# A conformer block and two mixer layers on one core: another order for the first block's transfers and steps, earlier tap sums, products of zeros at the start, and a last quarter taken token tile by token tile

## The chip, the core and the metric

The kernel runs on one core of a Trainium2 chip. The metric is the device time of one execution in microseconds (us), the median of several runs. TensorE (PE) multiplies, VectorE (DVE) and ScalarE (ACT) do the work on elements, GpSimd (POOL) does little here, and SyncE (SP) only issues transfers. Each of these engines takes its instructions in the order in which they are written.

## What is computed

A first block (conformer convolution and an MLP), then two layers of a second model, on 256 tokens of width 1024, in float32. The change touches the first block alone, up to its second pointwise product. Cut to that:

```python
mod = silu(c) @ w_mod + b_mod                        # w_mod 1024 x 6144, 24 MB
sh1, s1, g1, sh2, s2, g2 = split(mod, 6)
hl = rms_norm(x, norm1_g) * (1 + s1) + sh1
u = hl @ w_pw1 + b_pw1                               # w_pw1 1024 x 2048
a, gate = split(u, 2)
u = a * sigmoid(gate)
u = dwconv(u in 4 segments of 64, w_dw) + b_dw       # 31 taps
u = silu(layer_norm(u, ln_g, ln_b))
y = u @ w_pw2 + b_pw2
x = x + g1 * y
x = x + g2 * (square(relu((rms_norm(x, norm2_g) * (1 + s2) + sh2) @ w1)) @ w2)
```

## The kernel before

**Weights.** Every weight comes in one stream of transfers of up to 1 MB on SP's queue, in the order of a plan (`PLAN`). Weights that are split into a rounded part and a rest go into one of three `raw` buffers (2048 columns, so two chunks of 1024); ACT makes `hi` (L408), DVE makes `lo` (L425), and the last `lo` of a buffer frees it. `W.get` and `W.ahead` keep the split two chunks ahead of the products. The pieces of `w_mod` are not split; they go into one of four `home` buffers of 1 MB (home0, home1 and the two halves of home2), and a home is free when its reader is done. SP issues in the plan's order: a transfer whose buffer is not yet free holds back every one behind it.

**The modulation.** F0 to F3 (two transfers each) hold the columns of sh1 and s1 for a quarter of the channels, D0 to D3 those of s2, P0 to P7 those of g1 and sh2, R0 to R3 those of g2. F, P and R are multiplied on PE (`mod_chunk`, four products of 32 rows, L744). ACT then copies the row (`modrow`, L754), and small products turn it into columns (`mod_columns`, `mod_cols`). D is multiplied and summed on DVE (`mod_dots`, two instructions, L782).

**The first pointwise product.** The 16 chunks c0 to c15 each hold two blocks of 128 x 512. A block is multiplied for two token tiles t with three products each (L915 to L917): 12 products per chunk, accumulated in `gated[q][t]` for the four column quarters q. Chunks 0 to 11 go channel pair by channel pair over q = 0, 1, 2 and need the modulated input of F0, F1, F2, F3 in turn (`modulated(c)`, called M); chunks 12 to 15 are q = 3. When a quarter has its last block, `glu(q)` (ACT `sg`, DVE L873) frees its banks and starts `conv`: products `x_ps` (L890), DVE products with the tap sums `wf` (L893), products `c_ps` (L897), a copy to `cb` (L902) and statistics (L903).

**Order.** Two strings set it: `TRANSFERS` the plan's first part, `PW1_STEPS` the order of steps. Generators in `bg` are advanced by one at each `slot()`. After the steps come P6, P7 and R0 to R3, then the layer norm of `cb`, eight transposes with SiLU (`ln_act`), and the second pointwise product `pw2` (L700 to L702): four steps of 24 products, then `finish`.

**Tap sums.** `tap_sums` (two products L821, each followed by an ACT copy L822) runs behind c0. Its source row is then overwritten by `c_row`, which the dots need.

Of the kernel before, what the change touches and what calls it, by code (L numbers as in the profile page):

```python
# [27 lines left out]
RANK = 1 + 3 * NFREQ  # L28
# [14 lines left out]


TRANSFERS = (
    "F0 c0 F1 c1,2 c3 F2 c4,5 D0 F3 c6,7 P0 D1 c8,9 P1 D2 c10,11 P2 P3 D3 c12,13 P4 P5 c14,15 P6 P7 w0,1 R0 R1 w2,3 R2 R3 "
    "w4,5,6,7"
)
PW1_STEPS = (
    "c0 F1 c1 M1 c2 c3 F2 c4 M2 c5 D0 c6 F3 c7 M3 c8 P0 D1 c9 P1 D2 c10 P2 c11 D3 P3 c12 P4 c13 P5 c14 c15"  # L50
)


# [423 lines left out]
def tile_conformer_then_mixer(ctx: ExitStack, tc: tile.TileContext, stream, xT, pT, vec, con, rows_in, taps, c_row, out):  # L477
# [11 lines left out]
    def bank(name):  # L489
        return pp_.tile([P, 512], F32, tag="b", name=name)  # L490
# [59 lines left out]
    def slot():  # L550
        step(stages)
        step(bg)

    def drain():
        while bg:
            slot()
# [287 lines left out]
    normed(0, 2)  # L844
    for _ in work:
        pass
    pw1_bias(2)

    def modulated(c):
# [11 lines left out]
            nc.vector.tensor_sub(xs[:, k, T:], xn[:, k, :], xs[:, k, :T])  # L861

    modulated(0)
    normed(2, KB)

    czb = rows1[:, :D]


    def glu(q):
        for t in range(2):  # L870
            sg = tp.tile([P, T], F32, tag="t256", name="sg", bufs=6)
            nc.scalar.activation(sg, gated[q][t][:, 256:], AF.Sigmoid)
# [11 lines left out]
    def conv(t, c0, c1):  # L884
# [17 lines left out]
        nc.scalar.copy(cb[:, t, c0:c1], o[:, :n])  # L902
        nc.vector.bn_stats(stats[:, t, max(c0 // 256 - 1, 0), :], o[:, :n])  # L903

    def pw1_chunk(i):
        hi, lo = W.get(("pw1", 0, i))
        for j in range(2):
            q, k = PW1[2 * i + j]
            if k == 0 and q not in gated:
                pw1_bias(q)  # L910
            s = slice(512 * j, 512 * j + 512)
            for t in range(2):
                xh, xl = (xs[:, k, T * part + P * t : T * part + P * t + P] for part in range(2))
                kw = dict(start=False, skip_group_check=True)
                nc.tensor.matmul(gated[q][t], xh, hi[:, s], stop=False, **kw)  # L915
                nc.tensor.matmul(gated[q][t], xh, lo[:, s], stop=False, **kw)
                nc.tensor.matmul(gated[q][t], xl, hi[:, s], stop=(k == KB - 1), **kw)  # L917
# [22 lines left out]

    works = {}
    for item in PW1_STEPS.split():
        taken(item[0], int(item[1:]))
        if item == "c0":
            tap_sums()
            nc.sync.dma_start(czb, c_row.to_broadcast([P, D]))
        elif item == "c2":
# [54 lines left out]
    mv_ = tp.tile([P, 2, 2], F32, tag="lnmv", name="lnmv", bufs=1)
    rstd = tp.tile([P, 2], F32, tag="rt", name="rstd")
    for t in range(2):
        nc.vector.bn_aggr(mv_[:, t, :], stats[:, t].rearrange("p a b -> p (a b)"))
    rsqrt_(rstd, mv_[:, :, 1], 1.0)
    nc.scalar.preload_act_table_set("silu_and_others")
    for c in range(2):
        for t in range(2):
            part = cb[:, t, 512 * c : 512 * c + 512]  # L1010
            nc.vector.tensor_scalar(part, part, mv_[:, t, 0:1], rstd[:, t : t + 1], ALU.subtract, ALU.mult)
# [16 lines left out]
    pw2 = Mixed("pw2", 0, xs, PW2_EARLY, PW2_LATE, ev_pw2)  # L1028
    acts = {}

    def ln_act(k):
        ps = bank("tr_ps")
        for t in range(2):
            nc.tensor.transpose(ps[:, P * t : P * t + P], cb[:, t, P * k : P * k + P], ident)
        n = acts[k] = tp.tile([P, T], F32, tag="t256", name="lnx", bufs=6)
        nc.scalar.activation(n, ps[:, :T], AF.Silu, scale=V("ln_g", k, 1), bias=V("ln_b", k, 1))

    for k in range(KB + 2):
        if k < KB:
# [12 lines left out]
        if j == 4:  # L1052
            bg.append(bias_rows())
# [667 lines left out]
```

## Time and profile before

| what | value |
|---|---|
| median of 3 runs | 1061.83 us (1057.67 to 1063.64) |
| the profiled execution, its own time | 1061.67 us |
| its span, first to last instruction | 1059.9 us |
| PE busy | 1015.3 us, 96% |
| DVE busy | 752.7 us, 71% |
| ACT busy | 593.0 us, 56% |
| DMA | 192.9 MB, mean 182 GB/s |

A busy PE is not PE at its best: the page also gives the clock that it was granted, and its products take about twice as long at the lower of two levels. The chain of waits is followed back from the last instruction; its rows tell which work ended last in each stretch. For a transfer two things count: when SP could issue it, and how long it took to land.

### The profile page before, as it was taken

Reading aid. Unit: us, or ns where it says so; the run is one execution under the profiler, and the core shown is the slowest. Engines: PE = TensorE matmul, PEld = TensorE weight load, DVE = VectorE, ACT = ScalarE, POOL = GpSimd, SP = SyncE. Lnnn points to the kernel's source line nnn. Section 1 sums busy time; section 2 is a strip of 40 time slices with the busy share of each in tenths; the row PEclk is TensorE's granted clock in tenths of the full one; section 3 lists DMA queues with packets and bytes.
Section 4 is the critical chain, followed back from the end, with each engine's and each line's share of the span. In section 5 each row is a group of like instructions: output and inputs, shape, how many; then the busy total and the mean of one; then the engine's idle time right before and its main releaser. Section 6 shows DMA issues by size and latency. Waiting matters only on the chain.

```text
span 1059.9 us, 16455 instructions
## 1 busy us (share of the span) xinstructions
PE 1015.3 (96%) x6386; PEld 875.8 (83%) x6386; DVE 752.7 (71%) x1445; ACT 593.0 (56%) x1070; POOL 101.8 (10%) x86
## 2 busy tenths in 40 slices
PE   6878899999999999999999999999999999999996
PEld 3554488988888989898888888998989888888896
DVE  5245347785788779886888875467997788887545
ACT  5332366553565644767555554674576765554555
POOL 0000004000003200002000002520000200000243
PEclk9888979999999999899999999999999999999998
DMA  9669625555555543334555555454343455555541
GB/s 375 257 267 368 267 93 185 209 198 175 186 192 168 181 154 106 126 131 140 194 197 199 180 179 198 155 188 132 140 147 122 134 190 194 195 174 187 198 160 40
DMA packets 28416, 192.90 MB, mean 182 GB/s; under 512 B 3368, under 2 KB 3757, under 8 KB 6961
## 3 DMA queue, kind: packets, MB, share of 16 engines
q1 hardware_dynamic: 26784, 188.32, 49.6%
q0 software_dynamic: 784, 1.99, 0.7%
q10 hardware_dynamic: 770, 1.54, 0.4%
q8 instruction: 50, 0.82, 0.3%
q14 instruction: 28, 0.23, 0.1%
HBM read 190.78 MB, written 2.04 MB: 182 GB/s over the span
## 4 chain that ended last, share of the span: by engine, by line
PE 77%; DVE 8%; ACT 4%; issue 1%; DMA 1%; DVEq 0%; ACTq 0%
PE g_ps L638 33%; PE g_ps L639 17%; PE mx_ps L700 3%; PE mx_ps L702 3%; PE g_ps L631 3%; PE mx_ps L701 3%; PE g_ps L632 2%; PE g_ps L633 2%; DVE lo L425 2%; ACT hi L408 1%; PE o_ps L1380 1%; PE pt_ps L1417 1%; PE cs_ps L616 1%; DMA home<-stream 1%; DVE big_a L1358 1%
## 5 line engine op out<-in xcount | busy, mean ns | idle before, releaser
L408 ACT CAST hi<-raw 128x1024 fp32r<-128x1024 f32 (+2 forms) x310 | 320.5, 1036 | 308.1 <-PE g_ps L638 148.8
L425 DVE TENSOR_TENSOR lo<-raw,hi 128x1024 fp32r<-128x1024 f32 (+2 forms) x294 | 361.0, 1230 | 143.2 <-ACT hi L408 142.2
L638 PE MATMUL g_ps<-xf,hi 128*128 128x512 f32 x704 | 247.0, 395 | 0.0
L639 PE MATMUL g_ps<-xf,lo 128*128 128x256 f32 x704 | 197.4, 280 | 0.0
L638 PEld LDWEIGHTS g_ps<-xf,hi 128*128 128x128 f32 x704 | 132.0, 187 | 30.9
L639 PEld LDWEIGHTS g_ps<-xf,lo 128*128 128x128 f32 x704 | 133.0, 189 | 0.1
L638 PE MATMUL g_ps<-big_f,hi 128*128 128x512 f32 x352 | 124.4, 397 | 0.0
L639 PE MATMUL g_ps<-big_f,lo 128*128 128x256 f32 x352 | 99.1, 281 | 0.0
L638 PE MATMUL g_ps<-big,hi 128*128 128x512 f32 x256 | 90.5, 397 | 0.0
L638 PEld LDWEIGHTS g_ps<-big_f,hi 128*128 128x128 f32 x352 | 66.1, 188 | 16.3
L639 PE MATMUL g_ps<-big,lo 128*128 128x256 f32 x256 | 72.1, 282 | 0.0
L638 PE MATMUL g_ps<-xs_h,hi 128*128 128x512 f32 x192 | 67.0, 393 | 0.0
L639 PEld LDWEIGHTS g_ps<-big_f,lo 128*128 128x128 f32 x352 | 66.4, 189 | 0.0
L638 PEld LDWEIGHTS g_ps<-big,hi 128*128 128x128 f32 x256 | 48.1, 188 | 11.8
L639 PE MATMUL g_ps<-xs_h,lo 128*128 128x256 f32 x192 | 53.8, 280 | 0.0
L602 POOL TENSOR_TENSOR accP<-accP,sq 128x256 f32<-128x256 f32 x12 | 17.7, 1479 | 331.0 <-ACT sq L601 331.0
L639 PEld LDWEIGHTS g_ps<-big,lo 128*128 128x128 f32 x256 | 48.3, 188 | 0.1
L631 PE MATMUL g_ps<-xs_l,hi 128*128 128x256 f32 x144 | 42.9, 298 | 0.0
L638 PEld LDWEIGHTS g_ps<-xs_h,hi 128*128 128x128 f32 x192 | 36.0, 187 | 8.1
L632 PE MATMUL g_ps<-xs_l,lo 128*128 128x256 f32 x144 | 41.7, 290 | 0.7 <-DVE lo L425 0.7
L631 PE MATMUL g_ps<-xn,hi 128*128 128x256 f32 x144 | 41.8, 290 | 0.0
L633 PE MATMUL g_ps<-xs_l,hi 128*128 128x256 f32 x144 | 41.6, 289 | 0.0
(360 smaller groups left out, 2245.9 us busy)
## 6 DMA issues: line engine op xcount, KB each, us to landing
raw<-stream SPq DMA_DIRECT2D x142, 1024.0 KB, 4.8
home<-stream SPq DMA_DIRECT2D x24, 1024.0 KB, 8.6
raw<-stream SPq DMA_DIRECT2D x4, 904.0 KB, 4.5
raw<-stream SPq DMA_DIRECT2D x4, 768.0 KB, 4.5
raw<-stream SPq DMA_DIRECT2D x2, 896.0 KB, 4.4
raw<-stream SPq DMA_DIRECT2D x2, 784.0 KB, 4.3
h<-xT SPq DMA_DIRECT2D x1, 1024.0 KB, 6.7
raw<-stream SPq DMA_DIRECT2D x2, 512.0 KB, 11.4
```

Of the source, the lines that this page charges most:

```text
L408: self.nc.scalar.copy(hi[:, : PLAN[i][1]], raw)
L425: eng.tensor_sub(lo[:, :w], raw, hi[:, :w])
L602: nc.gpsimd.tensor_add(acc, acc, s)
L616: nc.tensor.matmul(ps[:, :T], ones, part, start=(i == 0), stop=(i == len(parts) - 1))
L631: nc.tensor.matmul(ps, hi, xs[:, k, :T], start=first, stop=False)
L632: nc.tensor.matmul(ps, lo, xs[:, k, :T], start=False, stop=False)
L633: nc.tensor.matmul(ps, hi, xs[:, k, T:], start=False, stop=last)
L638: nc.tensor.matmul(ps, hi, xs[:, k, :], start=first, stop=False, skip_group_check=True)
L639: nc.tensor.matmul(ps[:, :T], lo, xs[:, k, :T], start=False, stop=last, skip_group_check=True)
L700: nc.tensor.matmul(ps, hi[:, s], xs[:, k, :T], start=first and m < 4, stop=False, **kw)
L701: nc.tensor.matmul(ps, lo[:, s], xs[:, k, :T], start=False, stop=False, **kw)
L702: nc.tensor.matmul(ps, hi[:, s], xs[:, k, T:], start=False, stop=last, **kw)
```

## The change

- `TRANSFERS` and `PW1_STEPS` are written anew. F3 now comes before c6,7 and the D, P and R pieces later: between c7 and c12 the steps take D0 to D3, between c11 and c15 P0 to P3, behind c15 P4 to P7. The order in which a home is used is now the order in which it was filled.
- R0 to R3 are taken in a generator `gate1` among the products of `pw2`.
- `tap_sums` does both products first, behind the columns of F0 and ahead of c0, and copies later; the `c_row` transfer is written ahead of c0. Loading the rest of the constants moves from c7 to c4, the sigmoid of `c_row` from c2 to c5.
- At the start PE gets four products of zeros (128 x 512, `WARM`), whose result is not read, and DVE a memset for them.
- c15 is multiplied token tile by token tile (`pw1_last`); `glu(3)` starts behind the first, each tile's convolution behind its own gate, and each tile has its own norm (`token_norm`).

```diff
-    "F0 c0 F1 c1,2 c3 F2 c4,5 D0 F3 c6,7 P0 D1 c8,9 P1 D2 c10,11 P2 P3 D3 c12,13 P4 P5 c14,15 P6 P7 w0,1 R0 R1 w2,3 R2 R3 "
+    "F0 c0 F1 c1,2 c3 F2 c4,5 F3 c6,7 D0 c8,9 D1 D2 c10,11 D3 P0 c12,13 P1 P2 P3 c14,15 P4 P5 w0,1 P6 P7 R0 w2,3 R1 R2 R3 "
     "w4,5,6,7"
-    "c0 F1 c1 M1 c2 c3 F2 c4 M2 c5 D0 c6 F3 c7 M3 c8 P0 D1 c9 P1 D2 c10 P2 c11 D3 P3 c12 P4 c13 P5 c14 c15"
+    "c0 F1 c1 M1 c2 F2 c3 c4 M2 c5 F3 c6 c7 M3 D0 c8 c9 D1 c10 D2 c11 D3 P0 c12 P1 c13 P2 c14 P3 c15"
...
+    nc.vector.memset(u[:, 0, :512], 0.0)
+    idle_ps = bank("idle_ps")
+    for _ in range(WARM):
+        nc.tensor.matmul(idle_ps, u[:, 0, :P], u[:, 0, :512], start=True, stop=True)
...
+    sums = tap_sums()
+    next(sums)
     pw1_bias(2)
...
     modulated(0)
+    for _ in sums:
+        pass
     normed(2, KB)
...
+    nc.sync.dma_start(czb, c_row.to_broadcast([P, D]))
...
+            if q == 3:
+                bg.append(conv(t, 256 * q, 256 * q + 256))
             yield
...
+    def pw1_last(i):
+
+        hi, lo = W.get(("pw1", 0, i))
+        for t in range(2):
+            for j in range(2):
+                pw1_products(hi, lo, i, j, t)
+            if t == 0:
+                W.ahead()
+                bg.append(glu(3))
+            slot()
...
+    taken("P", 4)
     slot()
+    taken("P", 5)
     slot()
     taken("P", 6)
+    slot()
+    norm0 = token_norm(0)
+    next(norm0)
+    slot()
+    drain()
     taken("P", 7)
-    slot()
     work = mod_columns("pair", 2)
-    next(work)
-    taken("R", 0)
-    taken("R", 1)
-    slot()
-    slot()
-    taken("R", 2)
-    taken("R", 3)
...
+    def gate1():
+        taken("R", 0)
+        yield
+        taken("R", 1)
+        yield
+        taken("R", 2)
+        yield
+        taken("R", 3)
+        bg.append(mod_columns("one", 5))
...
+    bg.append(gate1())
     for k in range(KB + 2):
```

SP's queue from the row for the dots (`c_row`) on, before. Line 394 is the stream; home2 stands for both halves of the third home buffer. In this order the rows are D0 and F3a, F3b, c6,7, P0, D1, c8,9, P1, D2, c10,11, the constants, P2.

```order
L946 DMA big0_84<-c_row 128x1024
L394 DMA home2_93<-stream 128x2048 x2
L394 DMA home0_91<-stream 128x2048
L394 DMA raw13_311<-stream 128x2048
L394 DMA home1_92<-stream 128x2048
L394 DMA home2_93<-stream 128x2048
L394 DMA raw16_367<-stream 128x2048
L394 DMA home2_93<-stream 128x2048
L394 DMA home0_91<-stream 128x2048
L394 DMA raw19_396<-stream 128x2048
L952 DMA cons_81<-con 128x1664
L394 DMA home1_92<-stream 128x2048
```

The same stretch of SP's queue now: F3a and F3b, c6,7, D0, c8,9, D1, the constants, D2, c10,11, D3, P0, c12,13.

```order
L881 DMA big0_84<-c_row 128x1024
L395 DMA home2_93<-stream 128x2048 x2
L395 DMA raw12_247<-stream 128x2048
L395 DMA home0_91<-stream 128x2048
L395 DMA raw14_301<-stream 128x2048
L395 DMA home1_92<-stream 128x2048
L977 DMA cons_81<-con 128x1664
L395 DMA home2_93<-stream 128x2048
L395 DMA raw17_378<-stream 128x2048
L395 DMA home2_93<-stream 128x2048
L395 DMA home0_91<-stream 128x2048
L395 DMA raw20_435<-stream 128x2048
```

F3 moved ahead of D0, and P0 behind all four D; c12,13 stand behind P0, which takes D0's buffer.

DVE from the columns of M3 on, now. Line 426 makes `lo`, 788 is a dot (two for each D), 888 the product with the gate; raw14 holds c8,9, raw17 c10,11, raw20 c12,13.

```order
L426 TENSOR_TENSOR lo18_418<-raw14_301,hi18_404 128x1024
L781 TENSOR_TENSOR mods_116<-mod_cols_117,vecs_80 128x2x2
L864 SCALAR_TENSOR_TENSOR G1_146<-mods_116,vecs_80 128x2
L873 TENSOR_TENSOR xs_h1_90<-big0_84,xs_h1_90 128x256 x2
L788 SCALAR_TENSOR_TENSOR home0_91,mods_116<-home0_91,big0_84 128x1024 x2
L426 TENSOR_TENSOR lo21_451<-raw17_378,hi21_437 128x1024
L426 TENSOR_TENSOR lo22_467<-raw17_378,hi22_453 128x1024
L888 TENSOR_TENSOR big0_84<-g_ps_147,sg_469 128x256
L788 SCALAR_TENSOR_TENSOR home1_92,mods_116<-home1_92,big0_84 128x1024 x2
L888 TENSOR_TENSOR big0_84<-g_ps_148,sg_483 128x256
L426 TENSOR_TENSOR lo25_492<-raw20_435,hi25_475 128x1024
L888 TENSOR_TENSOR big0_84<-g_ps_153,sg_494 128x256
```

Behind these rows stand D2, a gate product, the `lo` of c13, a gate product, D3. Before, D0 stood ahead of the columns of M3 and D2 ahead of the `lo` of c12; now each stands behind.

PE at the end of the stretch, before: the last convolution, R0 to R3 (line 744, R0 and R1 on home0 and home1, R2 and R3 on home2), the columns of P, the transposes.

```order
L890 MATMUL x_ps<-big_84,cons 118x256 x4
L744 MATMUL mod_ps<-home_91,cz 32x512 x4
L744 MATMUL mod_ps<-home_92,cz 32x512 x4
L897 MATMUL c_ps<-big_84,cons 64x256 x4
L744 MATMUL mod_ps<-home_93,cz 32x512 x8
L761 MATMUL mod_cols<-cons,modrow 128x4 x4
L1034 MATMUL tr_ps<-cons,big_84 128x128 x6
L700 MATMUL mx_ps<-xs_ln,hi_631 128x256
```

Now, where line 750 with home_91, home_92 and twice home_93 is P4 to P7, and the last one on home_91 is R0.

```order
L907 MATMUL x_ps<-big_84,cons 118x256 x2
L750 MATMUL mod_ps<-home_91,cz 32x512 x4
L907 MATMUL x_ps<-big_84,cons 118x256 x2
L750 MATMUL mod_ps<-home_92,cz 32x512 x4
L914 MATMUL c_ps<-big_84,cons 64x256 x2
L750 MATMUL mod_ps<-home_93,cz 32x512 x4
L914 MATMUL c_ps<-big_84,cons 64x256 x2
L750 MATMUL mod_ps<-home_93,cz 32x512 x4
L767 MATMUL mod_cols<-cons,modrow 128x4 x4
L1076 MATMUL tr_ps<-cons,big_84 128x128 x6
L750 MATMUL mod_ps<-home_91,cz 32x512 x4
L706 MATMUL mx_ps<-xs_ln,hi_620 128x256
```

R1 to R3 moved in among the products of `pw2`, and the columns of P no longer stand behind an R.

## Rows read from the trace of the kernel before

**Rows 1.** The page's first line, and the clock granted to PE in 40 equal slices of the span, in tenths of the full one.

```profile
span 1059.9 us, 16455 instructions
...
PEclk9888979999999999899999999999999999999998
```

**Rows 2.** Busy time of each engine by stretch (us from the span's start: length; PE, PEld, DVE, ACT, POOL with their counts; then the granted clock, the DMA share and GB/s).

```profile
27.00:60.00 33.00, 28.93 (x137) 18.52 (x138) 11.81 (x18) 12.29 (x18) 0.00 (x0) 0.86 0.54 202
60.00:90.00 30.00, 23.12 (x102) 14.54 (x100) 10.80 (x17) 6.98 (x11) 0.00 (x0) 0.89 0.88 357
90.00:121.00 31.00, 27.75 (x102) 13.98 (x106) 17.61 (x29) 9.84 (x17) 0.00 (x0) 0.83 0.76 298
...
136.00:154.00 18.00, 18.00 (x115) 17.66 (x116) 6.94 (x11) 8.94 (x17) 0.00 (x0) 0.74 0.17 58
...
170.00:1059.00 889.00, 875.33 (x5706) 786.14 (x5706) 676.93 (x1309) 522.54 (x954) 95.69 (x76) 0.99 0.48 167
```

**Rows 3.** The chain of waits between 102 and 136 us: start, time that this piece took in the chain, what.

```profile
102.70 0.43 PE g_ps L916
...
104.66 0.99 PE mod_ps L744 x8
...
106.33 0.23 PE g_ps L917
...
107.26 1.92 PE c_ps L897 x8
...
115.45 1.01 PE c_ps L897 x8
...
120.78 1.90 PE mod_ps L744 x16
...
122.70 6.31 DMA home<-stream
...
129.06 1.06 PE mod_ps L744 x8
130.12 1.00 PE mod_cols L761 x8
...
133.46 0.95 PE tr_ps L1034 x2
...
135.80 0.58 PE mx_ps L700
```

**Rows 4.** SP's queue in order of time: start of the first issue, time to the end of the last one in the row, what is issued, how many. The first is the row for the dots; the homes in the others are D0, F3a and F3b; P0 and D1; P2, P3 and D3.

```profile
26.52 0.33 SPq L946 DMA_DIRECT2D big<-c_row  x1
29.16 13.24 SPq L394 DMA_DIRECT2D home<-stream  x3
...
42.97 16.22 SPq L394 DMA_DIRECT2D home<-stream  x2
...
75.60 5.05 SPq L394 DMA_DIRECT2D home<-stream  x3
```

**Rows 5.** What SP's issues waited for in the first 160 us: total us, times, longest.

```profile
SPq L394 <- PE mod_ps L744: 54.5, 10, 13.6
SPq L394 <- DVE home L782: 31.5, 4, 15.4
SPq L394 <- DVE lo L425: 30.7, 3, 22.9
```

**Rows 6.** Issues of transfers between 113.8 and 114.2 us, with what is moved, its size and the us from issue to landing: one, with nothing else under way.

```profile
home<-stream SPq DMA_DIRECT2D x1, 1024.0 KB, 4.8
```

**Rows 7.** The same between 29.0 and 29.3 us: D0, issued while `c_row` was still under way.

```profile
home<-stream SPq DMA_DIRECT2D x1, 1024.0 KB, 7.1
```

**Rows 8.** The stretch from 15 to 30 us, in which transfers followed each other without a gap (columns as in Rows 2).

```profile
15.00:30.00 15.00, 12.77 (x46) 6.04 (x45) 8.18 (x17) 5.70 (x10) 0.00 (x0) 0.75 1.01 418
```

**Rows 9.** The beginning in order of time: start, length, engine, line, what, in brackets the idle time before and what ended it. The first is F0 on PE, then the split of c0, the columns of F0, the first product with c0, the second tap sum, F1.

```profile
10.85 3.86 PE L744 MATMUL mod_ps<-home,cz 128*32 128x512 f32 x16
...
14.02 1.05 ACT L408 CAST hi<-raw 128x1024 fp32r<-128x1024 f32 x1 [2.31 <-DMA raw<-stream]
...
15.62 1.03 PE L771 MATMUL mod_cols<-cons,modrow 128*128 128x1 f32 x8
...
18.49 0.50 PE L915 MATMUL g_ps<-hi,xs_h 128*128 128x512 f32 x1 [0.73 <-ACT xs_h L856]
...
25.10 1.38 PE L821 MATMUL wf_ps<-big,cons 31*118 31x512 f32 x2 [0.68 <-ACT big L822]
...
27.16 3.64 PE L744 MATMUL mod_ps<-home,cz 128*32 128x512 f32 x16 [0.68 <-ACT big L822]
```

**Rows 10.** DVE's groups between 16 and 136 us: line, engine, operation, names and shapes, count, then busy us, mean ns of one, idle time before and what ended it.

```profile
L425 DVE TENSOR_TENSOR lo<-raw,hi 128x1024 fp32r<-128x1024 f32 x18 | 21.9, 1222 | 38.4 <-ACT hi L408 38.4
L782 DVE SCALAR_TENSOR_TENSOR home<-home,big 128x1024 f32<-128x1024 f32 x8 | 9.4, 1217 | 0.0
...
L873 DVE TENSOR_TENSOR big<-g_ps,sg 128x256 f32<-128x256 f32 x8 | 3.3, 420 | 10.7 <-ACT sg L872 10.6
...
L893 DVE TENSOR_TENSOR big<-x_ps,big 118x512 f32<-118x512 f32 x4 | 2.5, 679 | 0.0
```

**Rows 11.** ACT's groups of the same stretch, with the same columns.

```profile
L408 ACT CAST hi<-raw 128x1024 fp32r<-128x1024 f32 x17 | 17.6, 1045 | 49.2 <-DMA raw<-stream 39.9 <-issue 4.9 <-PE g_ps L917 4.4
L859 ACT ACTIVATE big<-big,mods,G 128x256 f32<-128x256 f32 x6 | 3.6, 599 | 6.6 <-DVE G L852 6.6
```

More of the change, by code (lines that the diff above doesn't have):

```diff
@@ L35 @@
 EPS = 1e-6
+WARM = 4
 NEG = -1.0e30
@@ L817, in tap_sums @@
     def tap_sums():
+        pss = [bank("wf_ps") for _ in range(2)]
         for c in range(2):
-            ps = bank("wf_ps")
-            nc.tensor.matmul(ps[:RANK], C("at")[:TAPS], rows1[:TAPS, 512 * c : 512 * c + 512], start=True, stop=True)
-            nc.scalar.copy(wf[:RANK, 512 * c : 512 * c + 512], ps[:RANK])
+            nc.tensor.matmul(
+                pss[c][:RANK], C("at")[:TAPS], rows1[:TAPS, 512 * c : 512 * c + 512], start=True, stop=True
+            )
+        yield
+        for c in range(2):
+            nc.scalar.copy(wf[:RANK, 512 * c : 512 * c + 512], pss[c][:RANK])
     for q in range(2):
@@ L876, in glu @@
             ln_exp()
-        if q > 0:
+        elif q > 0:
             c0 = 0 if q == 1 else 256 * q
@@ L903, in conv, with pw1_products @@
         nc.vector.bn_stats(stats[:, t, max(c0 // 256 - 1, 0), :], o[:, :n])
+    def pw1_products(hi, lo, i, j, t):
+        q, k = PW1[2 * i + j]
+        s = slice(512 * j, 512 * j + 512)
+        xh, xl = (xs[:, k, T * part + P * t : T * part + P * t + P] for part in range(2))
+        kw = dict(start=False, skip_group_check=True)
+        nc.tensor.matmul(gated[q][t], xh, hi[:, s], stop=False, **kw)
+        nc.tensor.matmul(gated[q][t], xh, lo[:, s], stop=False, **kw)
+        nc.tensor.matmul(gated[q][t], xl, hi[:, s], stop=(k == KB - 1), **kw)
     def pw1_chunk(i):
@@ L910, in pw1_chunk @@
                 pw1_bias(q)
-            s = slice(512 * j, 512 * j + 512)
             for t in range(2):
[L913 to L917, printed above, removed]
+                pw1_products(hi, lo, i, j, t)
             if k == KB - 1:
@@ L922, in pw1_chunk @@
             slot()
+    def pw1_last(i):
+        hi, lo = W.get(("pw1", 0, i))
+        for t in range(2):
+            for j in range(2):
+                pw1_products(hi, lo, i, j, t)
+            if t == 0:
+                W.ahead()
+                bg.append(glu(3))
+            slot()
     def taken(kind, i):
         if kind == "c":
-            pw1_chunk(i)
+            (pw1_last if i == 15 else pw1_chunk)(i)
         elif kind == "F":
@@ L943, in tile_conformer_then_mixer @@
         taken(item[0], int(item[1:]))
[L944 to L947, printed above, removed]
+        if item == "c4":
+            nc.sync.dma_start(cons[:, CON_FIRST:], con[:, CON_FIRST:])
+        elif item == "c5":
             nc.scalar.activation(u[:, 0, :], czb, AF.Sigmoid)
-        elif item == "c3":
+        elif item == "c6":
             nc.vector.tensor_mul(czb, czb, u[:, 0, :])
-        elif item == "c7":
-            nc.sync.dma_start(cons[:, CON_FIRST:], con[:, CON_FIRST:])
         elif item == "c10":
@@ L955, in tile_conformer_then_mixer, with token_norm @@
     nc.vector.tensor_add(mods[:, 4, :], mods[:, 4, :], V("b_mod", 4 * KB, KB))
+    mv_ = tp.tile([P, 2, 2], F32, tag="lnmv", name="lnmv", bufs=1)
+    rstd = tp.tile([P, 2], F32, tag="rt", name="rstd")
+    def token_norm(t):
+        nc.vector.bn_aggr(mv_[:, t, :], stats[:, t].rearrange("p a b -> p (a b)"))
+        rsqrt_(rstd[:, t : t + 1], mv_[:, t, 1:2], 1.0)
+        yield
+        for c in range(2):
+            part = cb[:, t, 512 * c : 512 * c + 512]
+            nc.vector.tensor_scalar(part, part, mv_[:, t, 0:1], rstd[:, t : t + 1], ALU.subtract, ALU.mult)
+    taken("P", 4)
     slot()
+    taken("P", 5)
     slot()
     taken("P", 6)
+    slot()
[3 more added lines that the diff above has]
+    drain()
     taken("P", 7)
-    slot()
     work = mod_columns("pair", 2)
-    next(work)
-    taken("R", 0)
-    taken("R", 1)
-    slot()
-    slot()
-    taken("R", 2)
-    taken("R", 3)
+    norm1 = token_norm(1)
+    next(norm1)
+    for n in (norm0, norm1):
+        for _ in n:
+            pass
     for _ in work:
         pass
-    drain()
-    bg.append(mod_columns("one", 5))
-    slot()
+    nc.scalar.preload_act_table_set("silu_and_others")
     biasr = cp.tile([P, 5, 384], F32, name="biasr")
@@ L999, in bias_tiles @@
             yield
[L1002 to L1011, printed above, removed]
     G2 = cp.tile([P, KB], F32, name="G2")
@@ L1029, in tile_conformer_then_mixer @@
     acts = {}
+    def gate1():
+        taken("R", 0)
+        yield
+        taken("R", 1)
+        yield
+        taken("R", 2)
+        yield
+        taken("R", 3)
+        bg.append(mod_columns("one", 5))
     def ln_act(k):
```

## The prediction

> **What bounds the kernel now.** I read the page's first lines, then the stretches, the chain of waits, and SP's queue. From 170 us on PE is busy 875.3 of 889 us at a clock of 0.99 [rows 2]: nothing in the change reaches that stretch. Ahead of it PE is busy 28.9 of 33, 23.1 of 30 and 27.8 of 31 us, at clocks of 0.83 to 0.89 [rows 2], and the slices in which the clock sags all but stop there [rows 1]. Nor is the memory at its limit: 202, 357 and 298 GB/s [rows 2], where 418 were moved in a stretch without gaps [rows 8]. SP held its queue: 54.5 us for products with w_mod, 31.5 us for dots, 30.7 us for `lo` [rows 5]. D0, F3a and F3b took 13.2 us to issue, P0 and D1 16.2 us [rows 4], while what stood behind them, c6,7 and c8,9, was what PE needed. The end of the stretch is a transfer too: the last R, 6.31 us in the chain, then its products, P's columns (1.00), norm, transposes, and `pw2` begins at 135.80 [rows 3]. So I work out when `pw2` begins in the new order, and what it then carries.
>
> **Prices.** A product of pw1 steps on by 0.23 us at 2.4 GHz and 0.43 us at 1.2 GHz, a piece of w_mod takes 0.99 [rows 3] and at the lower level 1.9 (3.86 for two) [rows 9]; a chunk is 12 x 0.23 = 2.8 us. `lo` 1.22, a dot 1.22 (2.4 for a D), a gate product 0.42, a product with the tap sums 0.68 [rows 10], `hi` 1.05 and the modulating step 0.60 [rows 11]. A lone transfer of 1 MB lands 4.8 us after its issue [rows 6]; behind another, 1.049 MB at 418 GB/s [rows 8] is 2.5 us later.
> By the Trainium skill, "DMA: Bandwidth & Descriptors", section Specifications, the memory gives a core 358 GB/s, which would make this 2.9 us, by which the eight transfers of 1 MB from F3a to c10,11 would take some 3.4 us more (an estimate). Rows 8 measured 418, and the measurement decides.
>
> **The start.** Four products of zeros are new. The trace has no such product; 128 x 512 in f32 lies between 1.0 us (a `c_ps` pair of 512 takes 1.92 for four, two side by side [rows 3]) and 2.0 at half the clock, so 4 to 8 us from about 1.5 us on. At best they lift the clock and F0 takes 2 x 0.99 and not 3.86 us; at worst they end at 9.5, the eight bias products at 0.43 behind them end at 12.9, and F0 starts 2 us late. Neither decides: F0's columns wait behind ACT's `hi` of c0, which ends at 15.1 because its transfer came then [rows 9]. I take 0, with -0.3 and +2 us as ends.
> By the Trainium skill, "TensorE: Matmul & The Clock Gate", section Why this matters for your kernels, full throughput is had by keeping TensorE busy without a break; by that rule F0's two pieces gain 1.9 us, and the wait for c0 [rows 9] takes them back.
>
> **Tap sums.** Before, the second waited 0.68 us for the first's copy and began at 25.10, and F1 waited as long for the second's and began at 27.16 [rows 9]. Now both stand ahead of c0, 2 x 1.0 us in PE's wait for the input (0.73 us idle at 18.49 [rows 9]). They hold the last banks, so one bias product waits for a copy; c0 begins near 20.0 and not 18.5, and ends at 23 (24.5 at the lower clock). F1 follows at once: 4 us gained. `c_row` is issued near 18.8 and not 26.52 [rows 4], hidden behind c4,5.
>
> **The middle, on PE.** From 23 on every step has its data: F1 25, c1 27.8, M1's columns 28.7, c2 31.5, F2 33.5, c3 and c4 39, M2 39.9, c5 42.7, F3 44.7, c6 and c7 50.2, M3's columns 51.1, c8 53.9. The transfers keep up: behind c4,5 at 30.2 come `c_row` 31.4, F3 33.9 and 36.4, c6,7 38.9, D0 41.4, c8,9 43.8, D1 46.3, constants 48.2, D2 50.7, c10,11 53.1, D3 55.6. Before, c6,7 stood behind F3b, issued just before 42.4 [rows 4], so they landed near 42.4 + 4.8 + 2.5 = 49.7. But D0 once took 7.1 us and not 4.8 [rows 7], beside `c_row`; with such a lag, 2.3 to 3.9 us, c6 to c11 come that much later, and all below with them.
>
> **Where the new order waits.** DVE is the link. M3's columns stand behind the `lo` of c9, near 52.2; ACT's and DVE's steps for two channel groups take 2.8 (the columns 0.3, then 2 x 0.60 and three steps of 0.42, as long as a gate product of the same size [rows 10, 11]); then D0, done at 57.4. Only then may P0 go, in D0's home, and c12,13 stand behind P0: 57.4 + 4.8 + 2.5 = 64.7. Its `hi` holds up the next gate on ACT, so its `lo` ends at 67.7; a gate, D2 (2.4) 70.5; a gate, `lo` of c13, a gate, D3 74.9. P3 takes D3's home, c14,15 stand behind P3: 74.9 + 4.8 + 2.5 = 82.2, and their `lo` ends at 84.5. The products with the tap sums stand behind that `lo` on DVE, and `c_ps` on PE behind them. PE is through with c13's first half by 79, so it idles there for 5 to 10 us and starts again at the lower clock.
> From 84.5: two tap products 1.4, `c_ps` 3.8 and `x_ps` 2.0 (twice 1.92, and twice the 1.01 of a quarter's `c_ps` [rows 3]) at the lower clock, half of c13 1.6, P2 1.0, c14 2.8, `c_ps` 1.0, P3 1.0, c15 2.8: 101.9. Then the last quarter: `x_ps` and `c_ps` 2.0, P4 to P7 4.0, the row's copy 0.6 (as ACT's other steps), columns 1.0, and from the transposes to the first product 2.3, as from 133.46 to 135.80 [rows 3]: `pw2` begins at 112. P4 to P7 cover the gates and statistics of the two tiles; without that cover some 3 us would show. With the lag it begins at 116. I take 114, 21.8 us ahead of 135.80 [rows 3].
>
> **In pw2.** R1 to R3 are now there, 3.0 us; R's columns go to a later place. P's homes come free between 104 and 108, so R0, w2,3 and R1 to R3 land 2.5 us apart behind P7, R3 near 118 to 121, about when PE is at it. Before, from 136 to 154 the clock was 0.74 [rows 2], so about half of these 18 us ran at the lower level, some 4.7 us lost; now PE comes from P4 to P7 and R0 with shorter gaps, and I count 1.7 to 3.4 lost. Net 1 us later (-0.5 to +2.5).
> Sum: 21.8 - 1.0 = 20.8. The profiled execution took 1061.67 us (span 1059.9), 0.16 below the median of 1061.83, so it stands for it: 1061.67 - 20.8 = 1040.9, forecast 1041. Its own range, from lag, start, clock and R's: 1036 to 1046.
>
> **Rivals.**
> - *The waits for D and R cost more.* Each D is a link between DVE and SP's queue, and an R that lands late stops PE inside `pw2` with nothing behind it. For it: dots held SP up to 15.4 us at once [rows 5]. Against: only one D now stands behind a late `lo`. If P0 comes 4 us later than worked out and an R stops PE for 4 us: 1049.
> - *No lag, no low clock.* If the clock stays up from c0 on (1.5), after the idle stretch (2.7) and in `pw2` (1.7), and no transfer lags (2): 1033. Against: the clock sagged in every such gap before.
> - *The change does not shorten the stretch.* If c14,15 came only as before, P, c15 and R would end where they did, within 0.5% of before, which is about what a measurement of this kernel can tell from no change. It needs some 21 us more on DVE's chain than I find.
> - *Slower: PE at the lower clock throughout.* Work of some 70 us at 2.4 GHz lies between 23 and 112, with about 15 us of waits to absorb it. Before, 0.86, 0.89 and 0.83 in the stretches from 27 to 121 [rows 2] put some 26 of 94 us at the lower level (twice what the clock lacks of 1). If more than 45 us of that work ran at 1.2 GHz, `pw2` would begin beyond 141 and the kernel take over 1067; all of it: about 1095. Against: that is more than in all of these stretches together, though PE waited longer in them.
>
> **How the numbers follow.** Forecast 1041: 0.62. First rival 1049 (1046 to 1055): 0.19. Second 1033: 0.10. No change: 0.05. Slower: 0.04. The range leaves out the last two and the outer halves of the first two rivals: 1033 to 1052. Faster by over 0.5%: 0.91; within: 0.05; slower: 0.04.
>
> **What would show it.** In the profile after: F1 on PE near 23; no wait of PE ahead of c6; c6,7 landed by 43; D0's dots done at 57 to 61; P0 issued then; c14,15 landed at 82 to 86; PE idle ahead of `c_ps` for 5 to 10 us, ended by DVE's tap products; the first `mx_ps` at 111 to 117; no R in the chain of waits there; from `w1` on the same rows as before, 21 us earlier. It would be wrong if D0 is late, if PE's clock stays low between 23 and 55, or if an R ends the wait inside `pw2`.

## The result, and the profile after

| kernel | median us | ratio to the kernel before on the same chip (95% interval) |
|---|---|---|
| before, four executions (the three of the table above and one more) | 1062.3 (1057.67 to 1063.64) | |
| changed | 1044.99 (1043.73 to 1047.23) | 0.9847 (0.9812 to 0.9882) |

The changed kernel is 17.3 us faster by the medians, 16.2 by the means, of which the ratio is formed; the forecast was 20.8, its range 1033 to 1052 holds the time.

The page of the changed kernel: the first line, and PE's granted clock in 40 slices.

```profile
span 1042.7 us, 16472 instructions
...
PEclk7987999999999999999999999999999999999999
```

Its stretches; from 153 us on stands the work that had stood from 170 on.

```profile
27.00:60.00 33.00, 32.48 (x170) 23.81 (x166) 16.70 (x26) 18.89 (x27) 0.00 (x0) 1.00 0.87 354
60.00:90.00 30.00, 20.11 (x55) 10.07 (x55) 15.84 (x26) 4.42 (x8) 0.00 (x0) 0.70 0.66 252
90.00:121.00 31.00, 29.56 (x171) 13.89 (x174) 13.80 (x30) 13.35 (x25) 0.00 (x0) 0.96 0.69 261
...
153.00:1042.00 889.00, 875.15 (x5706) 785.97 (x5706) 677.16 (x1308) 522.31 (x954) 95.47 (x76) 0.99 0.48 167
```

Against [rows 2] PE is busy for the same time in the last row, to 0.2 us, so the gain lies ahead of it. From 27 to 60 us PE now works 32.5 of 33 us at full clock (28.9 at 0.86 before). From 60 to 90 it stands for 10 us and runs at 0.70: there the gain that was forecast is missing. The first product of `pw2` comes at 118.94 instead of 135.80 [rows 3], 16.9 us earlier, and from it to the end of the span pass 1042.7 - 118.94 = 923.8 us, 924.1 before (1059.9 - 135.80).

Where the 16.9 us came from shows in one stretch of each kernel, from F0's columns to the first product of `pw2`. The kernel before, then the changed one:

```profile
15.60:135.80 120.20, 99.58 (x444) 56.56 (x443) 52.84 (x96) 40.70 (x64) 0.00 (x0) 0.85 0.75 296
```

```profile
15.40:118.90 103.50, 91.64 (x419) 53.13 (x418) 52.99 (x95) 40.17 (x65) 0.00 (x0) 0.86 0.77 302
```

PE is idle for 11.9 us instead of 20.6 (8.8 less) and busy for 91.6 instead of 99.6 (7.9 less; R1 to R3 have left the stretch). The mean clock is the same: what was won in the middle was lost again at the start and between 68.5 and 92.4, where it was high for 3.4 us only.

PE's waits from 20 us to `pw2`: engine, tile and line, what ended the wait, us, times, longest. Before, the four longest:

```profile
PE mod_cols L771 <- ACT modrow L754: 5.3, 1, 5.3
PE g_ps L915 <- ACT xs_h L860: 3.9, 1, 3.9
PE g_ps L815 <- DVE big L873: 3.2, 1, 3.2
PE tr_ps L1034 <- DVE big L1011: 2.4, 1, 2.4
...
```

After, up to 130 us, so that the last row stands inside `pw2`:

```profile
PE x_ps L907 <- DVE big L888: 9.3, 1, 9.3
PE mod_cols L767 <- ACT modrow L760: 1.3, 1, 1.3
PE g_ps L821 <- DVE big L888: 0.6, 1, 0.6
PE g_ps L928 <- DVE lo L426: 0.5, 1, 0.5
PE mod_ps L750 <- DMA home<-stream: 0.2, 1, 0.2
...
```

Many waits became one. Its parts, in order of time, first PE, then ACT, then DVE (start, length, line, what, in brackets the idle time before and what ended it):

```profile
72.53 3.35 PE L907 MATMUL x_ps<-big,cons 64*118 64x512 f32 x6
85.20 2.05 PE L907 MATMUL x_ps<-big,cons 64*118 64x512 f32 x2 [9.31 <-DVE big L888]
...
83.36 1.04 ACT L409 CAST hi<-raw 128x1024 fp32r<-128x1024 f32 x1 [14.03 <-DMA raw<-stream]
84.31 0.38 ACT L887 ACTIVATE sg<-g_ps 128x256 f32<-128x256 f32 x1
...
84.72 0.42 DVE L888 TENSOR_TENSOR big<-g_ps,sg 128x256 f32<-128x256 f32 x1 [8.85 <-ACT sg L887]
85.06 1.22 DVE L426 TENSOR_TENSOR lo<-raw,hi 128x1024 fp32r<-128x1024 f32 x1
86.19 2.48 DVE L910 TENSOR_TENSOR big<-x_ps,big 118x512 f32<-118x512 f32 x4
```

Read from below: the fourth `x_ps` product pair needs a bank (a buffer in PSUM in which products are summed), and the bank still holds the third quarter's second token tile, whose gate product waits for its `sg`. That it is the bank is inferred: this pair reads only columns of the first two quarters, and the pair ahead of it, with the same columns, did not wait. On ACT that `sg` (0.4 us of work) is written behind the `hi` of c14, and ACT waits 14 us for the transfer of c14,15. So a gate that could have run at about 73 us ran at 84.3, and half of c12, P1 and half of c13, all of whose data were there, stood on PE behind it.

The same queue stood in the kernel before, where `sg` ran at 99.51 us behind the `hi` of c14 at 98.56; it cost little there, since c14,15 had landed at 98.46, just before PE came to that pair:

```profile
100.40 1.58 PE L890 MATMUL x_ps<-big,cons 64*118 64x512 f32 x2 [1.45 <-DVE big L873]
```

The changed kernel's path in the chain of waits (start, its share in us, what), up to the last R:

```profile
84.72 0.44 DVE big L888
85.20 2.05 PE x_ps L907 x2
...
90.11 1.87 PE mod_ps L750 x8
...
93.80 1.92 PE c_ps L914 x8
...
108.54 0.62 PE x_ps L907 x4
...
115.00 11.52 DMA home<-stream
```

The last row is R3: it landed at 126.52 and PE needed it at 126.3. Against what was forecast it stands in the chain, with a wait of 0.2 us.

### The profile page after: what moved, and what is told of

It reads as the page before. It is cut to its first block, busy times and chain, and to the rows that moved or that the text cites. A ratio compares the mean times of both kernels' runs of the same rounds, so it can differ in the third digit from the quotient of the medians.

```text
span 1042.7 us, 16472 instructions
## 1 busy us (share of the span) xinstructions
PE 1011.0 (97%) x6394; PEld 870.1 (83%) x6394; DVE 753.6 (72%) x1446; ACT 592.8 (57%) x1072; POOL 101.6 (10%) x86
## 4 chain that ended last, share of the span: by engine, by line
PE 78%; DVE 8%; ACT 4%; DMA 1%; issue 1%; DVEq 0%; ACTq 0%
PE g_ps L644 33%; PE g_ps L645 17%; PE g_ps L637 3%; PE mx_ps L706 3%; PE g_ps L638 2%; PE g_ps L639 2%; PE mx_ps L707 2%; PE mx_ps L708 2%; DVE lo L426 2%; DMA home<-stream 1%; ACT hi L409 1%; PE mod_ps L750 1%; PE o_ps L1423 1%; PE cs_ps L622 1%; PE pt_ps L1460 1%
## 5 line engine op out<-in xcount | busy, mean ns | idle before, releaser
L644 PEld LDWEIGHTS g_ps<-xf,hi 128*128 128x128 f32 x704 | 132.0, 187 | 30.8
L644 PEld LDWEIGHTS g_ps<-big,hi 128*128 128x128 f32 x256 | 48.1, 188 | 11.8
```

The lines of the kernel that those rows point to most:

```text
L644: nc.tensor.matmul(ps, hi, xs[:, k, :], start=first, stop=False, skip_group_check=True)
```

## The experiments

**Theory:** the lists do what was worked out; the 5 us that are missing come from the order on ACT and DVE at c14, behind which ready PE work was queued, and from the lower clock after the wait. **Rival:** the landing of c14,15 itself, as the last of the linked transfers, sets the end, and the order of the rest is of no account.

The time of one and the same kernel differs by 2 to 10 us from execution to execution, and between the two profiles of the changed kernel all of that lies behind `pw2` (last section). The first product of `pw2` in the profile is steadier, as far as two profiles of one kernel tell: 118.94 in the first of the changed kernel, 118.97 in the second (**e11**). So both stand here, with the rest of the span behind that product.

| run | median us | ratio (interval) | `pw2` begins | from there to the end |
|---|---|---|---|---|
| changed | 1044.99 | 0.9847 (0.9812 to 0.9882) | 118.94 | 923.8 |
| e11, changed again | 1047.73 | 0.9858 (0.9834 to 0.9882) | 118.97 | 927.5 |
| e1, no zeros | 1044.96 | 0.9866 (0.9843 to 0.9890) | 118.72 | 923.1 |
| e2, taps behind c0 | 1049.68 | 0.9916 (0.9891 to 0.9942) | 122.91 | 923.9 |
| e3, old lists | 1054.06 | 0.9923 (0.9894 to 0.9951) | 126.28 | 928.6 |
| e4, c15 whole | 1047.12 | 0.9857 (0.9829 to 0.9886) | 120.29 | 924.8 |
| e5, R ahead of the norm | 1056.33 | 0.9940 (0.9920 to 0.9960) | 130.43 | 924.3 |
| e6, both gates together | 1046.36 | 0.9878 (0.9853 to 0.9903) | 115.88 | 929.0 |
| e7, and one pair of tap products earlier | 1038.93 | 0.9803 (0.9776 to 0.9830) | 112.24 | 925.4 |
| e8, and the other pair | 1037.85 | 0.9781 (0.9752 to 0.9811) | 111.39 | 928.5 |
| e9, and w0,1 ahead of P4 | 1033.46 | 0.9731 (0.9706 to 0.9757) | 106.83 | 924.7 |
| e10, changed, wait filled | 1045.81 | 0.9848 (0.9823 to 0.9873) | 115.72 | 926.3 |

**e1, without the zeros**

```diff
-    nc.vector.memset(u[:, 0, :512], 0.0)
-    idle_ps = bank("idle_ps")
-    for _ in range(WARM):
-        nc.tensor.matmul(idle_ps, u[:, 0, :P], u[:, 0, :512], start=True, stop=True)
```

> The changed kernel without the four products of zeros and their memset. Theory (zeros are worth nothing): F0's pieces take 3.9 us instead of 1.6 and 1.9, and c0 begins within 1 us of 21.1; first product of pw2 at 118 to 120, 1044 to 1046 us. Rival 1 (the zeros raise the clock usefully): c0 begins 1 to 2 us later, everything behind it too, 1046 to 1048. Rival 2 (they cost: the clock is high while the zeros run and low from 10.5 to 24.2 us, while c0 is multiplied): without them c0 ends 1.5 to 2 us earlier than 25.5, 1042.5 to 1043.5.

The theory held: the zeros are worth nothing. c0 began at 20.89 (21.07 with them) and `pw2` at 118.72. They only move the clock's first high stretch: with them it lies at 7.1 to 10.5 us, without them at 16.1 to 19.5.

**e2, the tap sums at their old place**

```diff
...
-    sums = tap_sums()
-    next(sums)
...
         if item == "c0":
+            tap_sums()
+            nc.sync.dma_start(czb, c_row.to_broadcast([P, D]))
```

> The changed kernel with the tap sums (and the transfer of the row for the dots) back behind c0, product, copy, product, copy. Theory (the start lies on one chain with the late wait, through F1, the columns of M3, D0, P0's issue and c12's landing): F1 begins 2 to 4 us later than 25.45 and the landing of c14,15 (83.26) and the first product of pw2 (118.94) move by as much: 1047 to 1049 us. Rival (the 9.3 us idle of PE ahead of 85.2 takes it up): the landing of c14,15 and pw2 stay, 1045.

As the theory said. F1 on PE, then how it stood in the changed kernel:

```profile
28.15 3.38 PE L750 MATMUL mod_ps<-home,cz 128*32 128x512 f32 x16 [0.68 <-ACT big L828]
```

```profile
25.45 1.92 PE L750 MATMUL mod_ps<-home,cz 128*32 128x512 f32 x16
```

F1 ended 4.2 us later, c14,15 landed 4.3 us later (87.53 against 83.26), `pw2` began 4.0 us later. The start lies on the chain through M3, D0, P0 and c12 in full; the wait at 85 us takes up none of it, since it moves along.

**e3, the old lists with the rest of the change**

```diff
 TRANSFERS = (
-    "F0 c0 F1 c1,2 c3 F2 c4,5 F3 c6,7 D0 c8,9 D1 D2 c10,11 D3 P0 c12,13 P1 P2 P3 c14,15 P4 P5 w0,1 P6 P7 R0 w2,3 R1 R2 R3 "
+    "F0 c0 F1 c1,2 c3 F2 c4,5 D0 F3 c6,7 P0 D1 c8,9 P1 D2 c10,11 P2 P3 D3 c12,13 P4 P5 c14,15 P6 P7 w0,1 R0 R1 w2,3 R2 R3 "
...
 PW1_STEPS = (
-    "c0 F1 c1 M1 c2 F2 c3 c4 M2 c5 F3 c6 c7 M3 D0 c8 c9 D1 c10 D2 c11 D3 P0 c12 P1 c13 P2 c14 P3 c15"
+    "c0 F1 c1 M1 c2 c3 F2 c4 M2 c5 D0 c6 F3 c7 M3 c8 P0 D1 c9 P1 D2 c10 P2 c11 D3 P3 c12 P4 c13 P5 c14 c15"
...
```

> The changed kernel with the two strings of before (and the constants, the sigmoid and the product of the row for the dots at their old places); zeros, early tap sums, the last quarter by tiles and R0 to R3 inside pw2 stay. Theory (the two lists carry more than half of the gain): the waits of before for c6 to c11 come back, c14,15 land some 8 to 12 us later than 83.3, first product of pw2 at 127 to 131, 1053 to 1057 us. Rival (most of the gain is R0 to R3 no longer standing ahead of pw2): pw2 at 121 to 124, 1047 to 1050.

c14,15 landed at 95.06, 11.8 us later, as expected. `pw2` began at 126.28, between the two, nearer to the theory's 127. The lists are worth 7.3 us of 16.9, less than half, so the theory missed in that; the other parts alone bring 9.5. The old waits are back (PE, rows with a wait between 44 and 66 us):

```profile
50.58 0.50 PE L927 MATMUL g_ps<-hi,xs_h 128*128 128x512 f32 x1 [3.80 <-ACT xs_h L872]
...
64.95 1.22 PE L777 MATMUL mod_cols<-cons,modrow 128*128 128x1 f32 x5 [4.96 <-ACT modrow L760]
```

**e4, the last quarter whole**

```diff
...
-        (pw1_last if i == 15 else pw1_chunk)(i)
+        pw1_chunk(i)
...
```

> The changed kernel with c15 multiplied whole, both gates and both convolutions of the last quarter behind it, and the norm behind both. Theory (the way by tiles is worth little, since P4 to P7 and the convolution cover the gates either way): first product of pw2 1 to 2.5 us later than 118.9, 1046 to 1047.5 us. Rival 1 (nothing): pw2 within 0.5 us. Rival 2 (the norm's chain of statistics, logarithm and exponential shows in full): 4 us later, 1049.

`pw2` began 1.35 us later: worth little, as expected.

**e5, R0 to R3 ahead of the norm**

```diff
     work = mod_columns("pair", 2)
+    next(work)
+    for n in range(4):
+        taken("R", n)
...
```

> The changed kernel with R0 to R3 taken behind P7, ahead of the norm, as before, and only their columns inside pw2. Theory (R3 lands at 126.5 and its transfer is then what pw2 waits for): first product of pw2 at 128 to 130.5 instead of 118.9, of which some 4 us come back since pw2 holds no R products: 1050 to 1053 us. Rival (R's homes come free earlier and R lands earlier): pw2 at 123 to 125, 1045 to 1047.

`pw2` began at 130.43, 11.5 us later, as expected; the time was above what I expected, since only 1.8 and not 4 us came back between that product and the column sum behind `pw2` (32.1 us, 33.9 in the changed kernel). In the chain of waits R3's transfer is the wall, as it was in [rows 3]:

```profile
114.82 9.90 DMA home<-stream
...
124.76 1.93 PE mod_ps L750 x8
126.70 1.80 PE mod_cols L767 x8
...
130.43 0.58 PE mx_ps L706
```

So R inside `pw2` is the largest single part once the lists are new. The parts (4.0, 7.3, 1.35, 11.5, 0) add up to more than 16.9, because an R that is waited for hides what the others save.

**e6, both gates of the third quarter together**

```diff
             if q == 3:
                 bg.append(conv(t, 256 * q, 256 * q + 256))
-            yield
+            if q != 2 or t == 1:
+                yield
```

> The changed kernel with both gates of the third quarter written one behind the other, so that ACT's second sg stands ahead of the hi of c14. Theory (PE's wait of 9.3 us at the last x_ps is the queue on ACT, and half of c12 behind it was kept waiting for nothing): c12's second half runs before the wait; the wait moves to the x_ps of the third quarter, whose banks come free with DVE's tap products behind the lo of c14 (86.3); 2 to 3 us less, 1042 to 1043, first product of pw2 at 116 to 117. Rival (only the landing of c14,15 counts): 1045, pw2 at 119.

By the profile the theory held (`pw2` at 115.88, 3.1 us earlier), and the wait went where it said:

```profile
86.08 2.99 PE L908 MATMUL x_ps<-big,cons 64*118 64x256 f32 x8 [10.02 <-DVE big L911]
```

The wait is no shorter than before; only the work behind it became less. The time, 1046.36, missed the theory's 1042 to 1043: here 929.0 us passed behind that product, 5.2 more than in the first profile of the changed kernel. By times alone e6 is not told apart from it.

**e7, the first pair of tap products ahead of the `lo` of c14, too (e6's edit stays)**

```diff
-            if j == 1:
+            if j == 1 and i != 12:
                 W.ahead()
             slot()
+            if j == 1 and i == 12:
+                W.ahead()
```

> The same, and DVE's tap products written ahead of the lo of c14 as well. Theory (nothing but this order on ACT and DVE holds P1, c13, both c_ps and P2 behind c14's landing): PE does them between 76 and 85, and behind the lo of c14 only c14, P3, c15 and the last quarter are left; P5 to P7 are issued some 8 us earlier as their homes come free; the first product of pw2 at 107 to 112, 1034 to 1038. Rival (the transfers of P5 to P7 and R0 become the end): pw2 at 114 to 117, 1040 to 1043. Rival 2 (no gain): 1045.

`pw2` at 112.24 and 1038.93 us, a little short of the theory, since the wait was halved and not gone: the third quarter's tap products were still behind the `lo` of c14.

```profile
80.23 1.07 PE L750 MATMUL mod_ps<-home,cz 128*32 128x512 f32 x8
...
87.41 3.68 PE L915 MATMUL c_ps<-big,cons 119*64 119x512 f32 x8 [4.53 <-DVE big L911]
```

**e8, both pairs**

```diff
-            if j == 1 and i == 12:
-                W.ahead()
+            if j == 0 and i == 13:
+                W.rest(14)
```

> The run with the tap products ahead of the lo of c14, and now the third quarter's tap products ahead of it too (the lo of c14 is written one step later). There PE still stood 4.5 us in front of c_ps, until 87.4 us, and did c_ps, half of c13, c_ps and P2 (7.5 us) behind that. Theory: these now run before c14 is split; c14 begins at 87 to 89 instead of 94.9, and the first product of pw2 at 104 to 107 instead of 112.2: 1031 to 1035 us. Rival (P6, P7 and R0 to R3 come too late, since their homes come free one by one): pw2 at 108 to 111 or a longer wait for R3 inside pw2, 1036 to 1039.

This missed. PE ran through to c15's end at 95.1 us, but then stood for 2.9 us, and the clock went to its lower level from 97.5 to 104.3. PE, ACT, DVE:

```profile
98.06 1.21 PE L908 MATMUL x_ps<-big,cons 64*118 64x256 f32 x4 [2.94 <-DVE big L888]
...
93.30 1.05 ACT L409 CAST hi<-raw 128x1024 fp32r<-128x1024 f32 x1 [5.80 <-DMA raw<-stream]
...
95.33 2.34 DVE L426 TENSOR_TENSOR lo<-raw,hi 128x1024 fp32r<-128x1024 f32 x2
97.59 0.75 DVE L888 TENSOR_TENSOR big<-g_ps,sg 128x256 f32<-128x256 f32 x2
```

It is the same trap one chunk on: the gate of the last quarter behind the split of w0, whose transfer (w0,1, behind P4 and P5) landed at 93.3. e8's figures, 111.39 and 1037.85 us, lie at or in the rival's ranges, but not for the rival's reason: PE waited for no P6, P7 or R.

**e9, w0,1 ahead of P4 and P5**

```diff
-... c14,15 P4 P5 w0,1 P6 P7 R0 ...
+... c14,15 w0,1 P4 P5 P6 P7 R0 ...
```

> The run with both quarters' tap products ahead of the lo of c14, and the first weights of w1 (w0,1) moved ahead of P4 and P5 in the plan. Without that move PE stood 2.94 us ahead of the last quarter's x_ps, until 98.06 us: the gate stood on DVE behind the lo of w0, whose transfer, behind P4 and P5, landed at 93.3; then the clock was low for 6.8 us. Theory: w0,1 lands by 88, the gate comes as soon as c15's first token tile is multiplied, the clock stays up: first product of pw2 at 105 to 107 instead of 111.4, 1031 to 1034 us. Rival (P7 and R3 land later than needed and PE waits there instead, ahead of P's columns or inside pw2): pw2 at 108 to 111, or R3's wait over 2 us, 1035 to 1038.

As the theory said. From c12 on no wait of PE ahead of P's columns is longer than 0.2 us; there it is 1.3, as in the changed kernel:

```profile
95.91 0.69 PE L908 MATMUL x_ps<-big,cons 64*118 64x256 f32 x4
...
103.65 1.06 PE L767 MATMUL mod_cols<-cons,modrow 128*128 128x4 f32 x8 [1.28 <-ACT modrow L760]
...
106.83 0.58 PE L706 MATMUL mx_ps<-xs_ln,hi 128*128 128x256 f32 x1
```

This kernel is faster than both: 1033.46 us, 14.3 less than the changed kernel on the same chip, 27.6 less than the kernel before. c14,15 landed at 85.2 here, 1.9 us later than in the changed kernel, and `pw2` began 12.1 us earlier: the rival, by which that landing sets the end, falls.

**e10, the wait of the changed kernel filled with products by zeros**

```diff
+            if c0 == 0 and t == 1 and s == 1:
+                for _ in range(9):
+                    nc.tensor.matmul(gated[3][1][:31], cz[:, 0, 1:], h[:, :2, :], start=False, stop=False, skip_group_check=True)
             nc.tensor.matmul(xp[s][:RANK, :n], C("bt")[r], u[r, t, c0:c1], start=True, stop=True)
```

> The changed kernel with nine products by zeros (31 x 512, added to a sum, which they leave as it is) written ahead of the x_ps at which PE waited 9.3 us, so that PE is busy through most of that wait. Theory (behind the wait PE runs at the lower level until 92.4 us because it had stood still, and this costs 3 to 4 us): with them the clock stays up, c12's second half, P1 and c13's first half take half the time, and the first product of pw2 comes at 115 to 116 instead of 118.9: 1041 to 1042.5 us. Rival 1 (the level falls anyway, or the zeros run over and hold x_ps up): pw2 at 118.5 to 120, 1045 to 1046. Rival 2 (nothing behind the wait is on the path that sets the end): pw2 unchanged with a clock that stays up.

The filling on PE and the product behind it, then the stretch behind the wait; after that the same stretch of the changed kernel:

```profile
75.92 7.91 PE L909 MATMUL g_ps<-h,cz 128*31 128x512 f32 x18
85.29 1.11 PE L910 MATMUL x_ps<-big,cons 64*118 64x512 f32 x2 [1.45 <-DVE big L888]
...
85.20:99.00 13.80, 13.54 (x62) 6.35 (x64) 8.62 (x14) 3.27 (x4) 0.00 (x0) 1.00 0.46 163
```

```profile
85.20:99.00 13.80, 13.63 (x43) 6.11 (x44) 7.41 (x12) 2.21 (x3) 0.00 (x0) 0.74 0.41 153
```

The clock stayed up (1.00 against 0.74), and `pw2` began at 115.72, 3.2 us earlier. That prices the lower clock after this wait. Its time is 1.9 us below that of e11 on the same chip, with intervals that overlap.

**e11, the changed kernel again**

> The changed kernel itself once more, beside the two others and the kernel before on one chip: 1043.5 to 1046.5 us, 15 to 18 less than before, the first product of pw2 within 1.5 us of 118.9, and behind pw2 the same work up to 3 us longer or shorter from one execution to the next, as far as the low stretches of the clock near 410 and 690 us and the pace between 835 and 960 us differ.

`pw2` and the low stretches came as expected; the median lies 1.2 us above the range that I gave. By the medians the change gained 13.4 us on that chip, below the 15 to 18 that I gave, and 17.3 on the first; the intervals of the two ratios overlap almost wholly.

## Why the prediction was right, and where its size was off

| step | forecast | measured |
|---|---|---|
| zeros | 0 (-0.3 to +2) | 0.2 (e1) |
| c0 on PE | 20.0 to 23 (24.5) | 21.07 to 25.45 |
| F1 ends | 25 | 27.4 (30.8 before) |
| c6,7 landed; PE waits for them | 38.9 to 43; no | 39.7; no |
| D0 done, P0 issued | 57.4, then | 58.7, 58.8 |
| D3 done, c14,15 landed | 74.9, 82.2 | 75.9, 83.3 |
| `lo` of c14 ends | 84.5 | 86.3 |
| from there to c15's end | 17.4 | 22.3 (108.54) |
| from there to `pw2` | 10.1 | 10.4 (118.94) |
| lag of transfers | 2 counted | none |
| R3 landed | 118 to 121 | 126.5 |
| from `pw2`'s first product on | 1.0 later | 0.3 earlier |

**Right:** the mechanism and the order of its links. D0 was done, P0 issued and c14,15 landed within 1.4 us of what was worked out; no transfer from F3 to c10,11 lagged (2.5 us for each of 1 MB). In e2, e4 and e5 the start, the last quarter and the R's paid what their places in the chain said; the lists (e3) paid 0.7 us less than the least expected.

**The failed step** is the sentence "PE is through with c13's first half by 79, so it idles there for 5 to 10 us" ahead of `c_ps`. PE stopped at 75.9, three steps earlier, at the last `x_ps`. The prediction had each gate's `lo` and dots on DVE in order, but did not ask on which side of the `hi` of c14 the second `sg` stood on ACT, nor who held the bank that the fourth `x_ps` pair needed. So the last `x_ps`, half of c12, P1 and half of c13 fell behind the wait: 22.3 us and not 17.4. Between the end of that `lo` and `c_ps` stood 7.5 us of this work; against them, the tap products (1.4) ran beside it, and `c_ps` and `x_ps` found the upper level again and took 4.0 us and not 5.8; the other 0.6 are small pieces. e6 to e8 took them out piece by piece, and e9 shows what is there when no such queue is left. The tap products that were forecast as the end of the wait ended at 88.7, before PE had come to `c_ps` (93.7). Of the signs that were named, these failed: F1 came at 25.45 and not near 23, PE's idle time stood ahead of `x_ps`, the first `mx_ps` came behind 117, and an R did end a wait inside `pw2`, if only of 0.2 us. The row of the kernel before that is shown above (1.45 us, at the same pair) was there to be read.

**The start** was 2.4 us late at F1's end and 1.8 at the `lo` of c14. Between 10.5 and 24.1 us the clock was at its lower level, where the second tap sum took 2.8 us with the bias products beside it, and c0 4.4 instead of 2.8. The lower level for c0 had been given as 24.5; c0 also began 1.1 late.

**Two errors of the other sign** were smaller. The lag of 2 us did not come: the 2 us counted for it hid a part of the miss, which is luck. And `pw2` did not become longer: R1 to R3 came into it (3.2 us), but its clock stayed at 1.00 until 137, where it had been 0.74 [rows 2]. From its first product to the column sum behind it pass 33.9 us, 34.1 before. Together, from the 112 without lag and with 0.3 from c15's end to `pw2`: 112 + 1.8 + 4.9 + 0.3 = 119.0, that is 16.9 us ahead of [rows 3] and not 21.8; with the 0.3 gained behind it 17.2 in the span, and not 20.8.

That 0.3 is a net of larger pieces, and luck too. Right behind the column sum the clock now stands low, where it had been high. The same work before, then in the changed kernel:

```profile
170.70:174.20 3.50, 3.50 (x26) 3.40 (x27) 2.75 (x6) 2.98 (x7) 2.41 (x5) 1.00 0.28 58
```

```profile
153.80:157.30 3.50, 3.50 (x14) 3.15 (x15) 2.65 (x6) 2.84 (x7) 2.56 (x5) 0.51 0.28 72
```

From the first product of `pw2` to the first product of the one that follows (`mx_ps` from `xs_h`) pass 40.1 us now and 38.7 before: 1.4 later, near the 1.0 forecast, but not for its reason. All profiles of variants of the changed kernel show this low stretch, save e4 and e9; why was not tried. The 1.4 us came back far behind the change, 1.5 of them near 417 us, where the profile of the kernel before has the clock low for 6.8 us and that of the changed kernel for 3.4; two more pieces of 2.3 us, of opposite sign, cancel (480 to 600 and 835 to 956 us of the changed kernel).

**The clock after the wait** was counted rightly as low; e10 gives 3.2 us for it. By the Trainium skill, "TensorE: Matmul & The Clock Gate", section Why this matters for your kernels, a break in TensorE's work lets the clock drop and steady work keeps it up. e10 agrees (0.74 without the filling, 1.00 with it). The zeros at the start do not: there the clock fell while PE worked on (last section).

Why the shares of e6 and e10 in the time are smaller than in the start of `pw2`: in their profiles the rest of the span was longer than in that of the changed kernel, and the traces show where. Of e6's 5.2 us, 2.3 lie between 835 and 956 us, 1.6 in a low stretch of the clock near 696 us and 1.4 in a longer one near 417 us (times of the changed kernel); of e10's 2.5 us, 2.3 lie between 835 and 956 us. At these places e11, the same kernel, differs from the changed kernel's first profile as well (last section). That the executions without a profile went the same way is not shown, so the medians of e6 and e10 stay unexplained to that extent.

## What to carry to other kernels

When a wait for a transfer can't be removed, list for every engine what is written behind the instruction that waits, and move ahead of it all that has its data, down to a 0.4 us activation: its late result can hold a PSUM bank, and the bank whole chunks of products. Follow banks like data: a product that needs a bank waits for the last reader of the tile that held it. Judge an edit of a few microseconds by the start of a fixed piece of work in the profile, not by the time alone, when the rest of the kernel varies by as much; and compare what comes right behind it, too, since the clock there may have changed.

## What the runs showed of the hardware that was not expected

**The clock fell under a busy PE.** Changed kernel, 7 to 10.5 us and 10.5 to 24.1 us:

```profile
7.00:10.50 3.50, 3.43 (x14) 1.66 (x17) 2.07 (x5) 2.28 (x6) 0.00 (x0) 1.00 1.01 421
10.50:24.10 13.60, 12.66 (x41) 6.58 (x34) 6.81 (x19) 7.41 (x12) 0.00 (x0) 0.50 1.02 420
```

PE had worked from 1.49 to 11.6 us with one break of 0.07 us, and was busy 12.66 of the next 13.6, at half the clock. What brought it down was not tried. The same rows show 420 GB/s again, as [rows 8].

**The same work took 121.0 or 123.3 us at the same granted clock.** One stretch of the second mixer layer from the same ACT instruction to the same one, in the changed kernel and in e11:

```profile
834.60:955.60 121.00, 121.00 (x699) 106.56 (x699) 102.72 (x174) 70.48 (x128) 0.00 (x0) 1.00 0.54 190
```

```profile
836.10:959.40 123.30, 123.30 (x700) 106.90 (x699) 102.78 (x174) 70.46 (x128) 0.00 (x0) 1.00 0.53 187
```

PE is busy throughout, the granted clock reads 1.00 in both, and 2.3 us lie between them, spread evenly. The shorter time stands in the profiles of e1, e2 and e9 as well, the longer one in the other eight, the kernel before among them. Another 1.5 us came in e11 from a low stretch of the clock at 696 us that the first profile has not. The cause of neither was found; together they make up the 3.8 us by which the spans of the two differ (smaller differences, such as a low stretch near 417 us in the first profile alone, cancel).
